# End of the second products: the folds of the row sums behind the last chunk's first four column blocks

## The chip, the cores and the metric

The kernel runs on one core of a Trainium2 chip. The metric is the device time of one execution in microseconds (us); where several runs are given, their median. A profile is one execution recorded by the hardware profiler. Engines: TensorE (PE; its weight loads are shown apart as PEld), VectorE (DVE), ScalarE (ACT), GpSimd (POOL), SyncE (SP). SP, ACT and POOL also issue DMA transfers, each into queues of its own.

## The reference

Two layers run over 256 tokens of 1024 channels. The change lies in the second half of a layer, a lookup of 16,384 small experts. Each of 8 heads chooses 16 experts for a token and gives each a gate; an expert is one row of `expert_down` (dot product with the token, then GELU) and one row of `expert_up` (scaled by the result and summed):

```python
        u = expert_down[experts]
        act = jax.nn.gelu(jnp.einsum('td,thkd->thk', t, u, preferred_element_type=jnp.float32),
                          approximate=False)
        wgt = (gate * act).astype(t.dtype)
        vv = expert_up[experts]
        return jnp.einsum('thk,thkd->td', wgt, vv)
```

The result times a modulation vector is added to the residual stream: `x = x + g2 * peer_ffn(...)`. Then the next layer starts with a norm and the product with `w_in`; behind layer 1, x is the output.

## The kernel before

**Dense and row tokens.** The first T tokens (`DENSE`: 168 in layer 0, 160 in layer 1) are computed densely, as if every expert were used, with zero gates for those not chosen. For the other TS = 88 or 96 tokens the chosen rows are fetched from memory by indirect DMA. `SETS` splits these tokens into sets of 64, 16 and 8 (layer 0) or 64 and 32 (layer 1).

**Second products.** `combine` (line 1165) makes the weighted sum of `expert_up`. `up` stands in 128 chunks of 128 experts by 1024 channels, 512 KB each, loaded in turn into a ring of 7 buffers (`raw`), odd chunks by SP's queue and even ones by ACT's. A chunk's product is eight matmuls in f32, one for each column block d of 128 channels: `add(i, d, u)` (line 1172) adds chunk i's block d for T tokens. The accumulators `acc` are four PSUM tiles; each holds two column blocks side by side, d and d + 1, of 256 columns each: T for the dense tokens, the rest for the row tokens. The profile shows two records for each f32 matmul on TensorE, and two weight loads.

**Row sums.** Meanwhile POOL fetches rows of `up` (line 1074), and DVE adds each, times its weight, to `R_SUM[s]` of its set (`add_row`, lines 1097 and 1099). A partition of `R_SUM[s]` holds a part of one token's rows. `folds(d)` (line 1176) sums these parts: for each set a matmul with block d of `R_SUM[s]` as weights and a constant 0/1 matrix `fold` of as many columns as the set has tokens (line 1179). It writes beside the dense tokens' columns in the same accumulator. The work is given out so that the last row is added, in program order, ahead of chunk 123.

**Order at the end.** The part is issued in the order in which it is written (`manual_schedule`), and every engine takes its instructions in that order. Chunks 0 to 125 run whole, chunk by chunk. Behind chunk 125 stand all eight `folds(d)` (lines 1212 to 1214): 24 matmuls in layer 0, 16 in layer 1. The last two chunks (`HELD` = 2) are loaded and kept in `last`; then, for each column block d, chunk 126's and chunk 127's matmuls follow one another (lines 1215 to 1217). At i = 127 of layer 0 two steps of the next layer's weights are taken (`cast_step`, a cast on ACT and, in one of them, a subtraction on DVE).

**Behind it.** `updates` (line 390) gives eight DVE operations, one for each d, which read acc and add the product with the gate to x (line 392). In layer 0 they are run at the start of the next layer's `bridge` (line 424): DVE updates x, ACT makes `R_U` and squares from it, and TensorE starts the next layer's products (`multiply`, line 446) with `R_U`. In layer 1 they are run at the very end (lines 1353 to 1357), with output DMAs from SP behind d = 3, 5, 6 and 7.

Of the kernel before, what the change touches and what calls it, by code (L numbers as in the profile page):

```python
# [20 lines left out]
DC = 8  # L21
# [39 lines left out]
ASIDES_UP = (4, 100)  # L61
F_FIRST = 4
F_LAST = 124
HELD = 2
FILL = 1.5
FILL_DOWN = (2.2, 2.1)
EARLY = (112, 116, 96, 100, 64, 68)
# [15 lines left out]
def hybrid_trunk(ctx: ExitStack, tc: tile.TileContext, x_in, c_in, vec_in, w_ada, w_in, w_out, w_pq,  # L83
# [164 lines left out]
    def cast_step(late=None):  # L248
        k = Src.cast
        if k >= len(Src.seq):  # L250
            return False
        dma_ahead(k + 1)
        while Src.later and Src.ring[Src.later[0][0]] <= Src.ring[k + 1] - 1 + RAW - QUEUE_LAG:
            nc.scalar.dma_start(*Src.later.pop(0)[1:])
        kind, _, arg = Src.seq[k]
        raw = raws.pop(k)
        Src.cast += 1
        if kind == "aside":
            Src.asides.append((k, lambda: ada_chunk(arg[0], arg[1], raw)))
        elif kind == "ada":  # L260
            ada_chunk(arg[0], arg[1], raw)
        elif kind in ("whole", "early", "second"):
            ready.append((raw, None))
        else:
            hi = stream.tile([P, D], F32R, name="hi", tag="hi", bufs=3)
            lo = stream.tile([P, D], F32R, name="lo", tag="lo", bufs=3)

            def low():
                if arg is None:
                    nc.vector.tensor_sub(lo, raw, hi.bitcast(F32))  # L270
                else:
                    nc.vector.scalar_tensor_tensor(lo, raw, arg, hi.bitcast(F32), op0=OP.mult,
                                                   op1=OP.subtract)

            with tc.high_priority(offset=AHEAD):
                if arg is None:
                    nc.scalar.copy(hi, raw)  # L277
                else:
                    nc.scalar.activation(hi, raw, AF.Copy, scale=arg)
                if late is None:  # L280
                    low()
                else:
                    late.append(low)
            ready.append((hi, lo))
        load_more(k)
        return True

    def run_aside(least=4):
        if Src.asides and Src.asides[0][0] <= Src.cast - least:
            Src.asides.popleft()[1]()  # L290
# [5 lines left out]
    def next_chunk(ahead=2, late=None):  # L296
        while len(ready) < 1 + ahead and cast_step(late):
            pass
        return ready.popleft()
# [71 lines left out]
    def bank(tag, bufs):  # L371
        return psum.tile([P, 512], F32, name=tag, tag=tag, bufs=bufs)
# [13 lines left out]
    def preload(func, after):  # L386

        nc.scalar.activation(spare, after, func, scale=0.0, bias=eps)  # L388

    def updates(acc, mod, g):  # L390

        return [lambda d=d: nc.vector.scalar_tensor_tensor(
            X[:, d, :], acc[d // 2][:, (d % 2) * S:(d % 2 + 1) * S], mod[:, g + d:g + d + 1], X[:, d, :],
            op0=OP.mult, op1=OP.add) for d in range(DC)]
# [125 lines left out]
    def tables(layer, after=None):  # L520
        if after is not None:
            for r in (R_BIAS, R_SW, R_SB):
                nc.scalar.copy(r[:, 0, 0:1], after)
        q = nc.gpsimd if layer == 0 else nc.sync
        q.dma_start(R_BIAS, rel_bias)
        q.dma_start(R_SW, sgu_w[layer])
        q.dma_start(R_SB, sgu_b[layer])
        return lambda: tables_rest(layer)
# [479 lines left out]
    def experts(layer, rest):  # L1008
# [59 lines left out]
        def fetch():  # L1068
            while free and len(held) < min(2 * TS, known_to[0]) and quota[0] > 0:
                quota[0] -= 1  # L1070
                n = len(held)
                k = n % TS
                held[n] = free.popleft()
                nc.gpsimd.indirect_dma_start(  # L1074
                    out=held[n], out_offset=None, in_=rows if n >= TS else down_rows[:, :],
                    in_offset=bass.IndirectOffsetOnAxis(ap=R_WHERE[:, k:k + 1].bitcast(U32), axis=0))
# [12 lines left out]
        def dot_acts(lo, hi):  # L1089
            nc.scalar.activation(R_DOTS[:, lo:hi], R_DOTS[:, lo:hi], AF.Gelu)  # L1090
            nc.vector.tensor_mul(R_DOTS[:, lo:hi], R_DOTS[:, lo:hi], pairs[:, 1, lo:hi])
# [73 lines left out]
        def combine(layer, late, dotted):  # L1165
            qg = None
            jobs = [(0, k) for k in range(dotted, TS)] + [(1, k) for k in range(TS)]
            acc = [bank("acc", 4) for _ in range(DC // 2)]
            added = 0
            last = []  # L1170

            def add(i, d, u):
                nc.tensor.matmul(acc[d // 2][:, (d % 2) * S:(d % 2) * S + T], u[:, d * P:(d + 1) * P], acts[:, i, :],  # L1173
                                 start=i == 0 and d % 2 == 0, stop=i == 127, skip_group_check=True)

            def folds(d):
                for s, (off, n) in enumerate(SETS):
                    at = (d % 2) * S + T + off
                    nc.tensor.matmul(acc[d // 2][:, at:at + n], R_SUM[s][:, d * P:(d + 1) * P], fold[layer][:, off:off + n],
                                     start=False, stop=True, skip_group_check=True)  # L1180

            free.extend(SLOTS_UP)
            fetch()
            for i in range(128):
                u = next_chunk()[0]
                while added < min(len(jobs), -(-len(jobs) * (i - F_FIRST + 1) // (F_LAST - F_FIRST))):
                    kind, k = jobs[added]
                    (add_row if kind else dot)(k)
                    added += 1
                    if not kind and k == TS - 1:  # L1190
                        dot_acts(dotted, TS)
                run_aside()
                if i == 126:
                    while Src.asides:
                        run_aside(1)
                if i == 127 and layer + 1 < DEPTH:
                    cast_step()
                    cast_step(late)
                if i >= 128 - HELD:
                    last.append((i, u))  # L1200
                else:
                    for d in range(DC):
                        add(i, d, u)
                if i == 120 and layer + 1 < DEPTH:
                    preload(AF.Sqrt, acts[:, i, 0:1])
                if i == 64 * S // T + 5:
                    nc.sync.dma_start(X.rearrange("p a b -> p (a b)"), x_dram)
                if i == 56 * S // T + 4 and layer + 1 < DEPTH:
                    others = tables(layer + 1)
                if i == 124 and layer + 1 < DEPTH:  # L1210
                    qg = others()
                if i == 125:
                    for d in range(DC):
                        folds(d)
            for d in range(DC):
                for i, u in last:
                    add(i, d, u)
            return updates(acc, mods[layer], G2), qg

        manual.enter_context(tc.manual_schedule())  # L1220
# [12 lines left out]
        start = None  # L1233
        for i in range(128):
# [46 lines left out]
            if start is None and shown == 2 and not lower:  # L1281
                start = i + 1
# [54 lines left out]
        if dotted < TS:  # L1337
            dot_acts(0, dotted)
        late = []
        update, qg = combine(layer, late, dotted)  # L1340
        return update, late, qg

# [95 lines left out]
```

## Time and profile before

| | |
|---|---|
| median of 3 runs | 1583.32 us (1582.72 to 1584.77) |
| the profiled execution, time | 1584.51 us |
| its span, first to last instruction | 1582.6 us |
| TensorE matmul / weight load busy | 1542.3 us (97%) / 1505.1 us (95%) |
| VectorE / ScalarE / GpSimd busy | 1000.0 / 472.5 / 496.8 us |
| memory read | 564.02 MB, 359 GB/s with what is written over the span |
| granted TensorE clock, mean | 0.991 of full |
| second products (L1173) | 4096 records, 580.5 us busy |
| folds (L1179) | 80 records, 48 in layer 0 and 32 in layer 1 |

How to read the views that follow. Times in a view count from the start of the span. The *chain of work that ended last* is followed back from the last instruction, at each step to what released it; a line is start, length, engine, tile, source line and how many instructions. The *timeline* lists instructions in order of time, like ones merged, with the idle time in front of them and what ended it in brackets. *Stretches* give, for a window, its length, then busy time and number of instructions of TensorE, its weight load, VectorE, ScalarE and, where it has any, GpSimd, then the granted TensorE clock (1.00 is full speed), the DMA engines' busy share and GB/s. *Groups* give engine, operation, output <- inputs, shape, count, then busy us and mean ns, then idle us before them. A *line's* view gives the shortest, median and longest duration in ns, then the first and the last start. In the *DMA queues*, q0 is the one of the row fetches, q1 is SP's and q10 is ACT's: packets, MB, share of the 16 engines' time. Matmuls overlap in TensorE's pipeline, so the pitch from one to the next is shorter than one's duration.

### The profile page before, as it was taken

To read this page: it belongs to the slowest core of one execution; us is meant where nothing else is said; L and a number is where in the kernel's file an instruction comes from. 1 tells how busy PE (TensorE), PEld (TensorE's weight loads), DVE (VectorE), ACT (ScalarE), POOL (GpSimd) and SP (SyncE) were. 2 spreads that over 40 slices of the span, in tenths; PEclk is the share of its full clock that TensorE was granted. 3 is DMA by queue.
4 is the path that set the end of the run, shared out by engine and by line. 5 is a ranking of instruction groups with operands and counts; after the bars stand their busy time and mean duration, and the time that the engine had idled before them with its cause. 6 is when DMAs were issued, how large, how long until landed. Compare 5 with 4: busy or idle time off the path is not lost.

```text
span 1582.6 us, 28957 instructions
## 1 busy us (share of the span) xinstructions
PE 1542.3 (97%) x11240; PEld 1505.1 (95%) x11240; DVE 1000.0 (63%) x2255; ACT 472.5 (30%) x1356; POOL 496.8 (31%) x424
## 2 busy tenths in 40 slices
PE   6999999999999999998999999999999999999997
PEld 5879999999999999998999899999999999999997
DVE  6778898677787444444337578877667754444434
ACT  2346313465553000000026663134656610000000
POOL 1000124334344434444200001245443334444441
PEclk9999999999999999999999999999999999999998
DMA  9998489999999999999955574899999999999995
GB/s 385 339 375 319 138 289 348 418 418 419 417 418 416 415 419 419 418 419 419 412 189 171 186 258 139 292 351 419 417 418 419 418 419 419 418 419 419 419 418 211
DMA packets 156681, 571.21 MB, mean 361 GB/s; under 512 B 18131, under 2 KB 18659, under 8 KB 155392
## 3 DMA queue, kind: packets, MB, share of 16 engines
q1 hardware_dynamic: 66096, 241.07, 39.7%
q0 software_dynamic: 55744, 202.36, 32.0%
q10 hardware_dynamic: 34704, 125.93, 19.9%
q8 instruction: 88, 1.44, 0.3%
q14 instruction: 49, 0.40, 0.1%
HBM read 564.02 MB, written 4.09 MB: 359 GB/s over the span
## 4 chain that ended last, share of the span: by engine, by line
PE 40%; DMA 38%; issue 8%; DVE 7%; POOL 4%; ACT 2%; ACTq 0%; POOLq 0%; SPq 0%; DVEq 0%
DMA arena<-in_up,arena 17%; PE acc L1173 17%; DMA arena<-in_down_rows,arena 12%; PE ch L357 9%; DMA spots<-in_down_rows,arena 3%; DMA raw<-in_up 3%; POOL arena L1074 3%; PE ch L359 2%; PE ch L360 2%; PE ch L361 2%; DVE raw L227 1%; DMA raw<-in_w_ada 1%; PE ch L446 1%; DVE arena L1084 1%; PE g L952 1%
## 5 line engine op out<-in xcount | busy, mean ns | idle before, releaser
L1173 PE MATMUL acc<-arena,raw 128*128 128x168 f32 (+1 forms) x4096 | 580.5, 305 | 9.0 <-DMA raw<-in_up 9.0
L1173 PEld LDWEIGHTS acc<-arena,raw 128*128 128x128 f32 x4096 | 577.6, 192 | 11.3 <-DMA raw<-in_up 11.2
L357 PE MATMUL ch<-arena,raw 128*128 128x168 f32 (+2 forms) x3776 | 560.7, 307 | 0.1
L357 PEld LDWEIGHTS ch<-arena,raw 128*128 128x128 f32 x3776 | 536.2, 190 | 5.6 <-issue 1.8
L1099 DVE SCALAR_TENSOR_TENSOR spots<-arena,spots 128x1024 f32<-128x1024 f32 x156 | 200.4, 1284 | 222.1 <-DMA arena<-in_up,arena 220.8
L1074 POOL DMA_INDIRECT arena<-in_up,arena x159 | 215.1, 1353 | 280.5 <-DMA arena<-in_up,arena 203.9
L1074 POOL DMA_INDIRECT arena<-in_down_rows,arena x151 | 178.3, 1181 | 242.9 <-DVE arena L1084 180.7
L1084 DVE SCALAR_TENSOR_TENSOR arena<-arena,spots 128x1024 f32<-128x1024 f32 x151 | 183.1, 1222 | 86.1 <-DMA arena<-in_down_rows,arena 79.6
L1117 ACT ACTIVATE arena<-arena,parts 128x128 f16<-128x128 f16 x164 | 64.6, 394 | 142.1 <-DVE arena L1107 102.5
L388 ACT ACT_TABLE_LOAD x6 | 7.7, 1283 | 284.9 <-PE acc L1173 284.8
L357 PE MATMUL ch<-arena 128*128 128x160 f32 (+2 forms) x544 | 86.0, 317 | 6.1 <-issue 3.6
L357 PEld LDWEIGHTS ch<-arena 128*128 128x128 f32 x544 | 79.8, 192 | 11.2 <-ACT arena L410 5.2
L1150 ACT ACTIVATE arena<-ch 128x336 f32<-128x336 f32 (+32 forms) x122 | 41.9, 343 | 149.4 <-PE ch L357 128.9
L227 DVE SCALAR_TENSOR_TENSOR aside<-aside,arena 128x1024 f32<-128x1024 f32 x48 | 58.6, 1220 | 43.9 <-DMA aside<-in_w_ada 43.8
L359 PE MATMUL ch<-hh,hi 128*128 128x256 f32 x288 | 82.6, 289 | 2.0 <-DVE arena L477 1.9
L360 PE MATMUL ch<-hh,lo 128*128 128x256 f32 x288 | 81.8, 284 | 0.0
L361 PE MATMUL ch<-hh,hi 128*128 128x256 f32 x288 | 81.7, 284 | 0.0
L270 DVE TENSOR_TENSOR lo<-raw,hi 128x1024 fp32r<-128x1024 f32 x42 | 51.2, 1225 | 37.3 <-ACT hi L277 36.3
L227 DVE SCALAR_TENSOR_TENSOR raw<-raw,arena 128x1024 f32<-128x1024 f32 x48 | 57.9, 1217 | 8.9 <-DMA raw<-in_w_ada 5.4
L1119 ACT ACTIVATE arena<-arena,parts 128x128 f16<-128x128 f16 x164 | 63.4, 387 | 0.0
L1123 ACT ACTIVATE arena<-arena,parts 128x128 f16<-128x128 f16 x164 | 63.4, 386 | 0.0
L1121 ACT ACTIVATE arena<-arena,parts 128x128 f16<-128x128 f16 x164 | 63.4, 386 | 0.0
(231 smaller groups left out, 1661.9 us busy)
## 6 DMA issues: line engine op xcount, KB each, us to landing
raw<-in_up SPq DMA_DIRECT2D x128, 512.0 KB
raw<-in_up ACTq DMA_DIRECT2D x128, 512.0 KB
raw<-in_down SPq DMA_DIRECT2D x114, 512.0 KB
raw<-in_down ACTq DMA_DIRECT2D x112, 512.0 KB
raw<-in_w_ada SPq DMA_DIRECT2D x48, 512.0 KB
aside<-in_w_ada SPq DMA_DIRECT2D x48, 512.0 KB
raw<-in_w_pq SPq DMA_DIRECT2D x32, 512.0 KB
arena<-in_down SPq DMA_DIRECT2D x30, 512.0 KB
```

Of the source, the lines that this page charges most:

```text
L227: nc.vector.scalar_tensor_tensor(raw, raw, 1.0, cact, op0=OP.mult, op1=OP.mult, accum_out=mods[layer][:, col:col + 1])
L357: nc.tensor.matmul(dst, hi[:, cols], k[0], start=start, stop=stop, **kw)
L359: nc.tensor.matmul(dst, hi[:, cols], k[0], start=start, stop=False, **kw)
L360: nc.tensor.matmul(dst, lo[:, cols], k[0], start=False, stop=False, **kw)
L361: nc.tensor.matmul(dst, hi[:, cols], k[1], start=False, stop=stop, **kw)
L1074: nc.gpsimd.indirect_dma_start(out=held[n], out_offset=None, in_=rows if n >= TS else down_rows[:, :], in_offset=bass.IndirectOffsetOnAxis ...
L1084: nc.vector.scalar_tensor_tensor(row, row, 1.0, R_DX[which(k)[0]], op0=OP.mult, op1=OP.mult, accum_out=R_DOTS[:, k:k + 1])
L1099: nc.vector.scalar_tensor_tensor(R_SUM[s], row, w, R_SUM[s], op0=OP.mult, op1=OP.add)
L1117: nc.scalar.activation(og[0][:, 0, i, :], oh[:, 0, i, :], AF.Copy, scale=parts[:, 0, t + i:t + i + 1])
L1119: nc.scalar.activation(og[1][:, 0, i, :], oh[:, 0, i, :], AF.Copy, scale=parts[:, 1, t + i:t + i + 1])
L1121: nc.scalar.activation(og[0][:, 1, i, :], oh[:, 1, i, :], AF.Copy, scale=parts[:, 0, t + 2 + i:t + 3 + i])
L1173: nc.tensor.matmul(acc[d // 2][:, (d % 2) * S:(d % 2) * S + T], u[:, d * P:(d + 1) * P], acts[:, i, :], start=i == 0 and d % 2 == 0, stop= ...
```

## The change

Chunks 126 and 127 are no longer held. Chunk 126 runs whole like those before it. Chunk 127 runs block by block; behind its blocks d = 4 to 7 stands `folds(d - 4)`, so behind block 4 the fold of block 0, and so on (`FOLD_LAG` = 4). Behind the last block stand `folds(4)` to `folds(7)`. The number of matmuls, their operands and shapes, the DMAs and the order of the other engines' instructions stay; the closing flag of an accumulation (`stop`) moves from the last chunk's matmuls to the folds alone, which now are the last to write each accumulator.

```diff
-HELD = 2
+FOLD_LAG = 4
...
-            last = []
-
             def add(i, d, u):
                 nc.tensor.matmul(acc[d // 2][:, (d % 2) * S:(d % 2) * S + T], u[:, d * P:(d + 1) * P], acts[:, i, :],
-                                 start=i == 0 and d % 2 == 0, stop=i == 127, skip_group_check=True)
+                                 start=i == 0 and d % 2 == 0, stop=False, skip_group_check=True)
...
-                if i >= 128 - HELD:
-                    last.append((i, u))
-                else:
-                    for d in range(DC):
-                        add(i, d, u)
+                for d in range(DC):
+                    add(i, d, u)
+                    if i == 127 and d >= FOLD_LAG:
+                        folds(d - FOLD_LAG)
...
-                if i == 125:
-                    for d in range(DC):
-                        folds(d)
-            for d in range(DC):
-                for i, u in last:
-                    add(i, d, u)
+            for d in range(DC - FOLD_LAG, DC):
+                folds(d)
```

## The prediction, made before the changed kernel was run

> **What bounds the kernel now.** I read the chain of work that ended last first, cut to the end of each layer's second products, then the timeline there, then the clock by stretches. Layer 0 of the two layers, chain (start us, us, what):
>
> ```profile
> 810.49 6.41 PE acc L1179 x48
> 816.90 6.82 PE acc L1173 x32
> 823.72 4.34 PE ch L446 x20
> ```
>
> Layer 1, the same view:
>
> ```profile
> 1564.33 1.30 DVE spots L1099
> ...
> 1565.67 6.61 PE acc L1179 x30
> 1572.28 6.09 PE acc L1173 x32
> ...
> 1578.40 0.48 DVE arena L392
> ```
>
> Both ends are a run of folds (L1179), then the 16 matmuls of the two held chunks (32 records: each f32 matmul leaves two), then the updates (L392). In layer 0, TensorE has no gap: it is the bound. In layer 1 the folds wait for DVE's last row sum. Timeline of layer 1:
>
> ```profile
> 1557.73 7.89 DVE L1099 SCALAR_TENSOR_TENSOR spots<-arena,spots 128x1024 f32<-128x1024 f32 x6 [0.30 <-DMA arena<-in_up,arena]
> ...
> 1560.83 0.33 PE L1179 MATMUL acc<-fold,spots 128*128 128x64 f32 x2
> ...
> 1565.67 6.61 PE L1179 MATMUL acc<-fold,spots 128*128 128x32 f32 x30 [4.51 <-DVE spots L1099]
> ```
>
> The first fold of the 64-token set goes at 1560.83, the first of the 32-token set stands 4.51 us, and both held chunks stand behind it. Last, busy time by stretch; after the POOL column comes the granted clock, then DMA share and GB/s:
>
> ```profile
> 810.33:814.35 4.02, 4.02 (x39) 4.02 (x38) 1.22 (x1) 2.19 (x3) 0.00 (x0) 1.00 0.66 217
> 814.35:821.17 6.82, 6.82 (x29) 6.82 (x29) 0.88 (x2) 1.26 (x3) 0.00 (x0) 0.50 0.19 68
> ...
> 1561.86:1565.27 3.41, 0.00 (x0) 0.00 (x0) 3.34 (x3) 0.00 (x0) 0.00 (x0) 1.00 0.07 29
> ...
> 1565.67:1572.00 6.33, 6.33 (x30) 6.33 (x30) 0.00 (x0) 0.00 (x0) 0.00 (x0) 0.50 0.00 0
> 1572.28:1578.37 6.09, 6.08 (x32) 5.84 (x32) 2.63 (x6) 0.00 (x0) 0.00 (x0) 0.73 0.07 29
> ```
>
> This is the second half of the price: the clock is at half through most of both ends. In layer 1 it falls behind an empty stretch of 3.41 us. In layer 0 it falls with TensorE busy, behind a stretch of folds alone. By shape, first the stretch before that fall (810.94 to 814.35), then one before another fall (749.50 to 752.91), then one after which the clock stayed (230.67 to 234.09); behind them, as before, two stretches with their clock:
>
> ```profile
> L1179 PE MATMUL acc<-fold,spots 128*128 128x64 f32 x11 | 2.4, 297 | 0.0
> L1179 PE MATMUL acc<-fold,spots 128*128 128x8 f32 x12 | 2.2, 256 | 0.0
> L1179 PE MATMUL acc<-fold,spots 128*128 128x16 f32 x10 | 1.7, 248 | 0.0
> ...
> L1173 PE MATMUL acc<-arena,raw 128*128 128x168 f32 x9 | 1.6, 323 | 2.5 <-DMA raw<-in_up 2.5
> ...
> L357 PE MATMUL ch<-arena 128*128 128x168 f32 x13 | 2.4, 312 | 1.6 <-issue 1.6
> ```
>
> ```profile
> 752.91:756.32 3.41, 3.41 (x15) 3.41 (x14) 1.28 (x1) 0.00 (x0) 1.43 (x1) 0.50 1.02 419
> 810.94:814.35 3.41, 3.41 (x33) 3.41 (x33) 1.22 (x1) 1.71 (x3) 0.00 (x0) 1.00 0.65 205
> ```
>
> A wide record costs 0.1427 us for 168 columns at full clock (1104 records below), 0.85 ns a column. So the folds' stretch streamed 11 x 64 + 12 x 8 + 10 x 16 = 960 columns, 0.82 of 3.41 us, a share of 0.24; the second 9 x 168 = 1512, 0.38; the third 2184, 0.54. My reading: the clock goes by streamed columns, and falls below a share somewhere between 0.38 and 0.54. This is an inference from few stretches.
>
> [...]
>
> **Costs.** Nothing is computed more or less: 80 fold records and 64 late records of chunks are moved. The speeds:
>
> ```profile
> 509.63 157.55 PE acc L1173 x1104
> ...
> 1524.83 36.16 PE L1173 MATMUL acc<-arena,raw 128*128 128x160 f32 x265
> ```
>
> At full clock an add record costs 157.55 / 1104 = 0.1427 us in layer 0 and 36.16 / 265 = 0.1365 in layer 1; a fold record 4.02 / 39 = 0.103 in layer 0. At half clock layer 1's folds cost 6.42 / 30 = 0.214 (1565.67 to the 1572.09 of the next group), so 0.107 at full. I take 0.105: the cost hardly follows the columns.
>
> *Layer 0.* Are the operands there? The row sums: the last add ends at 796.99. The chunks, by the last loads' issue, by the first weight cast of the next layer, which comes behind chunk 127 in the same queue, and by the DMA queues from 806 on:
>
> ```profile
> 795.71 1.28 DVE L1099 SCALAR_TENSOR_TENSOR spots<-arena,spots 128x1024 f32<-128x1024 f32 x1 [1.53 <-DMA arena<-in_up,arena]
> ...
> 810.45 1.04 ACT L277 CAST hi<-raw 128x1024 fp32r<-128x1024 f32 x1 [13.93 <-DMA raw<-in_w_in]
> ...
> L213 SPq DMA_DIRECT2D raw<-in_up x1: 328/328/328, 796.8 to 796.8; - x1
> L254 ACTq DMA_DIRECT2D raw<-in_up x1: 334/334/334, 801.4 to 801.4; - x1
> ...
> q1 hardware_dynamic: 652, 2.34, 40.2%
> ```
>
> From 806 to 824 the only traffic to speak of is SP's queue (q1), so ACT's (q10, chunk 126) had nothing left; in SP's queue, that of chunk 127, a later load had landed at 810.45. New order from 810.33: 32 add records x 0.1427 = 4.57, 48 fold records x 0.105 = 5.04, in all 9.6 us, to 819.9, if the clock stays. Now it is 13.39 us, to 823.72: gain 3.8. The 6.82 us at half clock are worth 3.41 by themselves; I take 3.6. What follows: the updates.
>
> ```profile
> 819.38 0.88 DVE L392 SCALAR_TENSOR_TENSOR arena<-acc,mod,arena 128x256 f32<-128x256 f32 x2 [6.63 <-PE acc L1173]
> ...
> 823.76 0.88 DVE L392 SCALAR_TENSOR_TENSOR arena<-acc,mod,arena 128x256 f32<-128x256 f32 x2 [0.26 <-PE acc L1173]
> ```
>
> They run in pairs, one pair to an accumulator, the last pair right behind TensorE's end. In the new order pair (0,1) is free after fold 1, four blocks early as now, and pair (6,7) after the last fold: the same shape, 3.6 us earlier, so the next layer's first products (L446) move with it. Released buffers: chunk 126's comes free at about 812.6 and not past 816, so SP issues further loads of the next layer earlier; DMA then stands still, as the row shows, so nothing collides and I count no gain.
>
> ```profile
> 816.90:823.72 6.82, 6.82 (x33) 6.82 (x34) 2.63 (x6) 2.98 (x8) 0.00 (x0) 0.69 0.00 0
> ```
>
> *Layer 1.* The row sum is done at 1565.63 as before (DVE and row fetches are untouched). Chunks landed? DMA queues from 1557 to 1566:
>
> ```profile
> q0 software_dynamic: 422, 1.51, 41.2%
> q10 hardware_dynamic: 4, 0.01, 0.2%
> ```
>
> Only row fetches (q0) move after 1557; ACT's queue has 4 packets left, SP's none: both chunks are there. From 1560.83: chunk 126 takes 16 records x 0.1365 = 2.18, chunk 127's blocks 0 to 4 take 10 x 0.1365 = 1.37, the first fold's 64-token part 0.21, to 1564.6; then TensorE waits about 1.0 us for the row sum. This is the wait that the change moves: queued behind it on TensorE are three blocks and the folds, and only the updates wait for these. From 1565.67: 30 fold records x 0.105 = 3.15 and 6 add records = 0.82, to 1569.6. Now it is 1578.37: gain 8.8 on TensorE. The stretch 1561.86 to 1565.27 is then mostly wide matmuls, so the fall at 1565.27 goes with its cause.
>
> ```profile
> 1576.22 0.88 DVE L392 SCALAR_TENSOR_TENSOR arena<-acc,mod,arena 128x256 f32<-128x256 f32 x2 [0.74 <-PE acc L1173]
> 1577.13 2.60 SPq L1357 DMA_DIRECT2D out_t<-arena  x4
> 1577.31 0.88 DVE L392 SCALAR_TENSOR_TENSOR arena<-acc,mod,arena 128x256 f32<-128x256 f32 x2 [0.21 <-PE acc L1173]
> ```
>
> The output starts behind update 3 (pair (2,3) ends at 1577.10). New: fold 3 ends at 1565.67 + 0.21 + 3 x (0.27 + 0.42) = 1567.95, its pair at about 1568.85: 8.25 earlier. Three pairs of 0.88 then stand back to back on DVE, the last ending at 1570.65, where now it ends at 1578.40 + 0.88 = 1579.28: 8.6. I take 8.3, the output's own length unchanged.
>
> **Sum:** 3.6 + 8.3 = 11.9 us. Off the profiled execution's own 1584.51 (its span is 1582.6) that is 1572.6; it lies 1.2 over the median of the runs, 1583.32, off which it is 1571.4. I take **1572.0**, between the two. Bounds of the unknown: the gain is 11.65 to 12.4 by the ends above, before the clock.
>
> **Rivals.**
>
> *One fall of the clock is left in layer 0.* The tail is 24 fold records alone, 2.5 us, before L446. A stretch of 3.41 us ending at the last fold has the tail (0.24) and one block with its fold (0.285 of adds, 0.63 of folds: 0.47), in all 0.30: a fall, if a window ends there. One ending a microsecond before or after is over 0.35, and where the windows lie is not set by the kernel as far as I can see. Price 3.41 / 2 = 1.7: 1573.7. [...]
>
> *Layer 0's part is lost*: the fold tail and the mixed blocks (share 0.47, inside my uncertain band) together hold the clock at half for two windows as now (3.41 lost), or the 3.6 us are waited for again in layer 1's DMA-bound stage. For: the band; against: that stage's loads start when layer 1's products release buffers, so they should move along. 11.9 - 3.6 = 8.3 left: 1575.6.
>
> *The last chunks are not there in layer 1* and TensorE waits for them instead. The latest that they can have landed is the end of all traffic:
>
> ```profile
> 1564.00:1565.00 1.00, 0.00 (x0) 0.00 (x0) 0.00 (x0) 0.00 (x0) 1.00 0.00 0
> ```
>
> From 1564.0, 32 add records (4.37) and 32 folds (3.36) end at 1571.7, not 1569.6: 1574.1. Against: the queue rows above.
>
> *Slower:* a fold between adds of the same accumulator does not overlap its neighbours.
>
> ```profile
> L1179 PEld LDWEIGHTS acc<-fold,spots x80: 190/306/338, 810.2 to 1571.8; 128*128 128x128 f32 x80
> L1179 PE MATMUL acc<-fold,spots x80: 219/352/454, 810.3 to 1571.9; 128*128 128x64 f32 x32, 128*128 128x16 f32 x16, 128*128 128x8 f32 x16, 128*128 128x32 f32 x16
> ```
>
> The ends for a fold record in the new place: 0.105, its pitch now, and 0.352, its whole median length. A weight load hidden under the add before it could also bring it below 0.105; the nearest such row, a wide record of 0.1427, has its own load hidden, and the folds' matmuls are too short to hide one, so I exclude a large gain. At 0.352, 48 + 30 records x 0.247 = 19.3 us: 1591.3. It decides from 0.105 + 11.9 / 78 = 0.26 us a record. Against: now adds of two chunks to the same columns follow each other without a gap, and so do three folds. I take 0.105, the pitch of the same instruction.
>
> **How the numbers follow.** Forecast 0.52, one fall 0.23, layer 0 lost 0.14, chunks late 0.04, slower 0.03, and 0.04 for what I have not seen, near no change. The range 1569.9 to 1575.8 reaches from the largest gain off the median, 1583.32 - 12.4 = 1570.9, less half the spread of the runs (1582.72 to 1584.77), to the loss of layer 0's part. About 0.2%, 3.2 us, can be told from no change: faster 0.94, within 0.03, slower 0.03.
>
> **What would show it.** In the chain, L1179 and L1173 mixed at both ends; granted clock 1.00 from 810 to the updates and from 1560 to the end of TensorE's work; about 1 us of wait for DVE L1099 in layer 1, not 4.5; from 810.33 (or its like) 9.6 us to L446; span near 1570.7. Clock at 0.50 in layer 0's tail shows the first or second rival; a wait for raw<-in_up the third; fold records further apart than 0.105 the last. The forecast is wrong if layer 1's start of the output moves by less than 8 us, or if layer 0's gain is not found again at the start of layer 1's second products.

## The result, and the profile after

The changed kernel takes 1573.74 us (median of 4 runs, 1573.04 to 1575.54); the kernel before, run beside it, 1584.05 us (4 runs, 1582.72 to 1585.47). The ratio is 0.9939 with a 95% interval of 0.9924 to 0.9954: 10.3 us less. Two later comparisons gave 0.9964 (0.9952 to 0.9977) and 0.9936 (0.9918 to 0.9953), so 5.6 and 9.5 us by their medians.

The profiled execution of the changed kernel spans 1571.1 us, before 1582.6. In its listing the adds stand on line 1171 and the folds on line 1177. The chain of work that ended last, layer 0:

```profile
769.96 41.33 PE acc L1171 x290
811.28 0.57 PE acc L1177 x6
811.85 0.39 PE acc L1171 x2
...
814.15 3.25 PE acc L1177 x30
817.40 6.13 PE ch L446 x20
...
```

Adds and folds alternate as the change says, and TensorE has no gap. But the 20 records of L446 now take 6.13 us, where they took 4.34 before. The clock by stretch shows why (windows of 3.41 us around the end of the folds; the granted clock is the third number from the end):

```profile
814.62:818.03 3.41, 3.41 (x29) 3.33 (x30) 2.35 (x6) 2.77 (x9) 0.00 (x0) 1.00 0.53 161
818.03:821.44 3.41, 3.41 (x10) 2.67 (x9) 3.41 (x10) 1.28 (x4) 0.00 (x0) 0.50 0.00 0
```

Of the 6.82 us at half clock before, 3.41 are left, moved from the folds to the next layer's first products. That is the first rival of the prediction, not its forecast. The forecast's sign, a granted clock of 1.00 from 810 to the updates, is not met.

In layer 1, from the timeline:

```profile
1554.24 6.67 DVE L1099 SCALAR_TENSOR_TENSOR spots<-arena,spots 128x1024 f32<-128x1024 f32 x5 [1.67 <-DMA arena<-in_up,arena]
...
1562.07 0.53 PE L1177 MATMUL acc<-fold,spots 128*128 128x64 f32 x4
...
1564.22 2.31 PE L1177 MATMUL acc<-fold,spots 128*128 128x64 f32 x20
1564.79 2.66 DVE L392 SCALAR_TENSOR_TENSOR arena<-acc,mod,arena 128x256 f32<-128x256 f32 x6 [0.56 <-PE acc L1177]
1565.69 2.32 SPq L1350 DMA_DIRECT2D out_t<-arena  x4
```

The last row sum is done at 1554.24 + 6.67 = 1560.91 and the first fold comes at 1562.07: in this execution TensorE does not wait at all. It came late, because it had waited for a chunk at the start of layer 1's second products, with a half-clock window behind it (timeline, then stretches):

```profile
1280.50 8.86 PE L1171 MATMUL acc<-arena,raw 128*128 128x160 f32 x64
1291.61 270.62 PE L1171 MATMUL acc<-arena,raw 128*128 128x160 f32 x1978 [2.26 <-DMA raw<-in_up]
```

```profile
1285.00:1295.00 10.00, 7.74 (x49) 7.50 (x48) 4.72 (x5) 0.00 (x0) 4.53 (x4) 0.87 1.03 417
1295.00:1305.00 10.00, 10.00 (x72) 10.00 (x72) 5.88 (x5) 0.00 (x0) 6.37 (x6) 0.96 1.03 415
```

Was that wait a price of the change? Did layer 0's gain reach the end? Is it the narrow folds that make the clock fall? The experiments ask these. Two measures serve throughout:

- **Layer 0's end:** from the end of chunk 125 to the end of L446's 20 records; it holds the folds, chunks 126 and 127 and these records, and nothing else. Before: 810.49 to 828.06, 17.57 us. Changed: 811.28 to 823.53, plus the 26 add records of chunks 126 and 127 ahead of the first fold, 26 x 0.1427 = 3.71: 15.96.
- **Layer 1's end:** from the last row sum to the end of the span. Before: 1565.63 to 1582.6, 17.0 us. Changed: 1560.91 to 1571.1, 10.2 us.

### The profile page after: what moved, and what is told of

Its sections match the earlier page's. It is cut to its first block, busy times and chain, and to the rows that moved or that the text cites. A ratio compares the mean times of both kernels' runs of the same rounds, so it can differ in the third digit from the quotient of the medians.

```text
span 1571.1 us, 28958 instructions
## 1 busy us (share of the span) xinstructions
PE 1535.6 (98%) x11240; PEld 1499.7 (95%) x11240; DVE 999.2 (64%) x2255; ACT 472.0 (30%) x1356; POOL 496.4 (32%) x424
## 4 chain that ended last, share of the span: by engine, by line
PE 72%; DMA 13%; issue 6%; DVE 4%; POOL 3%; ACT 2%; ACTq 0%; SPq 0%; POOLq 0%; DVEq 0%; another core or an unknown queue 0%
PE acc L1171 33%; PE ch L357 22%; DMA arena<-in_down_rows,arena 6%; DMA raw<-in_up 4%; POOL arena L1074 3%; PE ch L359 2%; PE ch L360 2%; PE ch L361 2%; PE g L1133 1%; DMA spots<-in_down_rows,arena 1%; DMA raw<-in_w_ada 1%; PE ch L446 1%; DVE raw L227 1%; PE g L952 1%; PE acc L360 1%
```

## The experiments

### The changed kernel again, and each layer alone

> The changed kernel once more. Theory A (the ends of the two layers carry the gain, and the wait of 2.3 us for chunk 4 at the start of layer 1's second products is a variation from run to run): again 10 to 11 us below the kernel before, with that wait sometimes there and sometimes not; one half-clock window of 3.4 us at the end of layer 0 in most executions. Theory B (the earlier start of layer 1 brings that wait with it): the wait of about 2.3 us at chunk 4 is there again, with a fall of the clock behind it.

Measured: 1576.64 us against 1582.22, ratio 0.9964 (0.9952 to 0.9977), 5.6 us, not the 10 to 11 that theory A expected. The wait at chunk 4 was not there, nor in the second repeat below; theory B falls for it. In its place stands the wait for the row sum, from the timeline of this run:

```profile
1562.92 0.33 PE L1177 MATMUL acc<-fold,spots 128*128 128x64 f32 x2
1565.13 0.41 PE L1177 MATMUL acc<-fold,spots 128*128 128x32 f32 x2 [1.88 <-DVE spots L1099]
```

The last row sum ends at 1565.09, the span at 1574.1: 9.0 us for layer 1's end. So the row sum is the bound in this execution. In the first profile TensorE came 1.2 us late for it (layer 1's end 10.2 us instead of 9.0): the early wait there took the place of this late one, and cost little beyond it.

> The new order in layer 0 alone; layer 1 keeps the folds behind chunk 125 and the held pair. Theory A: only layer 0's end is gained, 1.6 us with one fall of the clock on the next layer's first products, 3.4 us without, so 1.5 to 3.5 us below the kernel before; layer 1's end shows the wait for the last row sum and a half clock as before. Theory B: layer 0's gain is given back at layer 1's chunk 4 (2 to 3 us), so no difference within 1 us.

What differs from the changed kernel in this run and the next (here `NEW` = 0, there 1), cut to the order of the work:

```diff
-                for d in range(DC):
-                    add(i, d, u)
-                    if i == 127 and d >= FOLD_LAG:
-                        folds(d - FOLD_LAG)
+                if layer != NEW and i >= 128 - HELD:
+                    last.append((i, u))
+                else:
+                    for d in range(DC):
+                        add(i, d, u)
+                        if layer == NEW and i == 127 and d >= FOLD_LAG:
+                            folds(d - FOLD_LAG)
...
-            for d in range(DC - FOLD_LAG, DC):
+                if layer != NEW and i == 125:
+                    for d in range(DC):
+                        folds(d)
+            for d in range(DC - FOLD_LAG if layer == NEW else DC, DC):
                 folds(d)
+            for d in range(DC):
+                for i, u in last:
+                    add(i, d, u)
```

Measured: 1583.04 us against 1582.22, ratio 1.0 (0.9991 to 1.001, 11 runs). The time says B; the profiled execution (1580.18 us, one of the faster ones) does not. Its chain at layer 0's end:

```profile
810.81 0.57 PE acc L1181 x6
...
813.67 3.25 PE acc L1181 x30
816.92 6.13 PE ch L448 x20
```

With 3.71 us of adds ahead of 810.81 that is 15.95 us, 1.6 less than before. From there, 823.05, to the last row sum (1561.05) it is 738.0 us; before it was 737.6 and in a second profile of the kernel before (below) 738.0. So in this execution the layers' middle is not longer, and layer 0's gain is still there at the last row sum.

> The new order in layer 1 alone; layer 0 as before. Theory A: from the start of chunk 125 to the end of the span about 14.7 us instead of 23.9, so 8 to 9.5 us below the kernel before. Theory B: the same, and no wait at chunk 4 of layer 1, since layer 0 is as before; with B the gains of this run and of the run with layer 0 alone add up to the whole, with layer 0's part near zero.

Measured: 1577.73 us against 1582.22, ratio 0.9961 (0.9946 to 0.9976), with single runs from 1571.22 to 1581.66: 4.5 us by the medians, where A had 8 to 9.5. The profiled one is the slowest of them, and shows the layer 1 end that A left out, with a 2.33 us wait for the row sum inside one clock window:

```profile
1564.64:1568.05 3.41, 1.08 (x10) 0.94 (x8) 2.97 (x3) 0.00 (x0) 0.00 (x0) 1.00 0.03 12
1568.05:1571.46 3.41, 3.41 (x17) 3.41 (x16) 0.87 (x2) 0.00 (x0) 0.00 (x0) 0.51 0.00 0
```

TensorE was busy for 1.08 of 3.41 us, and everything behind ran at half clock: 12.0 us from the row sum (1567.69) to the end (1579.7), not 9.0. The change shortens the wait, but a rest of 2.33 us still cost 3 us of clock here; the 1.88 us of the first repeat did not.

### What makes the clock fall in layer 0

> The kernel before, with one matmul of 168 columns added behind each of layer 0's 24 folds (same weights, result unused). At full clock that is 48 more records of 0.1427 us, 6.85 us; the stretch from the first fold to the next layer's first product becomes 48 x 0.105 + 80 x 0.1427 = 16.5 us instead of 13.4. Theory A (the clock falls because the folds stream few columns; with the wide ones the share is about 0.67): the clock stays at 1.00 there, about 3 us slower than the kernel before. Rival (the fall belongs to the end of the part, whatever TensorE streams): the fall is there, 3.4 us more, about 6.5 us slower.

```diff
+            wide = bank("g", 2) if layer == 0 else None
...
+                    if layer == 0:
+                        nc.tensor.matmul(wide[:, :T], R_SUM[s][:, d * P:(d + 1) * P], acts[:, 125, :], start=True,
+                                         stop=True, skip_group_check=True)
```

Measured: one run of 1584.49 us; the kernel before beside it 1581.7, so 2.8 us slower. Stretches from the first fold to L446:

```profile
807.87:811.28 3.41, 3.41 (x29) 3.41 (x28) 1.23 (x1) 2.18 (x3) 0.00 (x0) 1.00 0.72 235
...
814.70:818.11 3.41, 3.41 (x29) 3.41 (x28) 0.00 (x0) 0.00 (x0) 0.00 (x0) 1.00 0.01 2
818.11:821.52 3.41, 3.41 (x28) 3.41 (x27) 0.11 (x1) 0.00 (x0) 0.00 (x0) 1.00 0.00 0
821.52:824.63 3.11, 3.11 (x24) 3.11 (x24) 2.51 (x6) 2.70 (x8) 0.00 (x0) 1.00 0.00 0
```

The clock is full throughout, with the DMA engines standing still as before. The stretch from 807.87 to 824.63 is 16.8 us where A had 16.5 and the rival 19.9. TensorE is 100% busy in both kernels; what differs is the columns that it streams. So in these runs the fall (granted clock 0.50 before, 1.00 with the wide matmuls) went with a run of narrow folds alone, not with the end of the part, with standing DMA engines or with TensorE's busy time.

> The changed kernel with every fold of layer 0 right behind its own block (lag 0); layer 1 keeps lag 4. The tail of 24 folds alone is gone; the stretch of chunk 127 with its folds has a share of streamed columns of 0.47 for 7 us. If the clock falls only below a share of about 0.4: no fall in layer 0, 1.7 us below the changed kernel. If it falls above 0.47: a fall inside the stretch, one or two windows, equal to the changed kernel or up to 1.7 us slower.

```diff
-FOLD_LAG = 4
+FOLD_LAG = (0, 4)
...
-                    if i == 127 and d >= FOLD_LAG:
-                        folds(d - FOLD_LAG)
+                    if i == 127 and d >= FOLD_LAG[layer]:
+                        folds(d - FOLD_LAG[layer])
...
-            for d in range(DC - FOLD_LAG, DC):
+            for d in range(DC - FOLD_LAG[layer], DC):
                 folds(d)
```

Measured: 1574.63 us against 1584.52, ratio 0.9939 (0.9921 to 0.9957); the changed kernel in the same comparison 1575.03. By time nothing is told apart. The chain of its layer 0:

```profile
811.28 0.57 PE acc L1177 x6
811.85 0.39 PE acc L1171 x2
...
817.97 0.57 PE acc L1177 x6
818.54 4.44 PE ch L446 x20
```

With the 18 add records ahead of the first fold (2.57 us) that is 822.98 - 811.28 + 2.57 = 14.27 us, 1.7 less than changed, and L446 is back at 4.44 us: no fall (granted clock 1.00 from 811.10 to 821.30). By shapes, one window of 3.41 us inside this stretch (814.51 to 817.92), and, from the second repeat of the changed kernel below, the window of its tail (815.50 to 818.91), behind which the clock fell (0.51 from 818.91 to 822.33):

```profile
L1171 PE MATMUL acc<-arena,raw 128*128 128x168 f32 x8 | 2.1, 348 | 0.0
L1177 PE MATMUL acc<-fold,spots 128*128 128x8 f32 x8 | 1.5, 256 | 0.0
L1177 PE MATMUL acc<-fold,spots 128*128 128x64 f32 x8 | 1.3, 247 | 0.0
L1177 PE MATMUL acc<-fold,spots 128*128 128x16 f32 x6 | 1.0, 249 | 0.0
```

```profile
L1177 PE MATMUL acc<-fold,spots 128*128 128x64 f32 x10 | 2.0, 281 | 0.0
L1177 PE MATMUL acc<-fold,spots 128*128 128x8 f32 x10 | 1.9, 265 | 0.0
L1177 PE MATMUL acc<-fold,spots 128*128 128x16 f32 x10 | 1.7, 249 | 0.0
L1171 PE MATMUL acc<-arena,raw 128*128 128x168 f32 x2 | 0.5, 348 | 0.0
```

At 0.85 ns a column (the prediction's 0.1427 us for 168) these are 2016 columns, a share of 0.50, and 1216, a share of 0.30. TensorE is busy without a gap in both (3.41 of 3.41 us). The closest case is the first profile of the changed kernel, with the window shown above (814.62 to 818.03), behind which the clock fell too:

```profile
L1177 PE MATMUL acc<-fold,spots 128*128 128x8 f32 x9 | 1.7, 256 | 0.0
L1177 PE MATMUL acc<-fold,spots 128*128 128x64 f32 x8 | 1.7, 288 | 0.0
L1177 PE MATMUL acc<-fold,spots 128*128 128x16 f32 x8 | 1.4, 249 | 0.0
L446 PE MATMUL ch<-arena,raw 128*128 128x257 f32 x4 | 1.3, 453 | 0.0
```

These are 1740 columns, a share of 0.43. The count takes every record whole that reaches into the window, so it is good to a few hundredths only.

### A layer 0 without a narrow tail

> Layer 1 as in the changed kernel. In layer 0 the folds stand behind chunks 123 to 125, three, three and two, and the last two chunks are held and run block by block, so that no stretch of folds alone and no narrow tail is left. If the clock goes by streamed columns (share 0.65 in the mixed chunks), it stays at full speed to the end of the next layer's first products: 1.7 us below the changed kernel. If the fall at the end of layer 0 has another cause (the end of the part, DMA standing still), it is there again and the time is that of the changed kernel.

```diff
-                if layer != NEW and i == 125:
-                    for d in range(DC):
+                if layer != NEW and 123 <= i <= 125:
+                    for d in range(DC)[3 * (i - 123):3 * (i - 122)]:
                         folds(d)
```

(Against the kernel with the new order in layer 1 alone: `NEW` = 1, and for layer 0 the held pair as in the kernel before.) Measured: 1572.5 us against 1582.22, ratio 0.9931 (0.9919 to 0.9944); the changed kernel beside it had 0.9964 (0.9952 to 0.9977). Its chain:

```profile
805.16 1.91 PE acc L1181 x18
...
814.98 4.66 PE acc L1175 x32
819.64 4.34 PE ch L448 x20
```

805.16 to 823.98 less the 32 records of chunks 124 and 125 (4.57) is 14.25 us: the full clock (1.00 in every stretch from 804.98 to 823.80), 1.7 us below the changed kernel, as A said. The medians differ by 4.1 us, more than that, so it was run again beside the changed kernel.

> The changed kernel once more, to be compared with the next three on one chip. Theory A (one fall of 3.4 us on the next layer's first products in layer 0; a wait of 0 to 2.5 us for the last row sum in layer 1, with or without a fall behind it; 0 to 4 us lost near 1085 us in every kernel): 6 to 10 us below the kernel before.

> Layer 0's folds spread over chunks 123 to 125, layer 1 as changed, once more. Theory A: layer 0 keeps its full clock, so 1.7 us below the changed kernel in the mean; the 4 to 5 us of the first comparison were mostly the varying spot near 1085 us. Rival (the spread does more than save one window, since it makes layer 1 start at another place): again 4 to 5 us below.

Measured: changed 1575.03 us, spread 1573.8, against 1584.52; ratios 0.9936 (0.9918 to 0.9953) and 0.9937 (0.9919 to 0.9955). In the profiles the differences are again those of A: layer 0's end 15.94 (changed) and, from the same lines as above, 14.25 (spread), layer 1's end 9.0 in both. In the time of whole executions, which vary by 5 us and more, 1.7 us does not show in this comparison; the rival's 4 to 5 us are not there.

> The kernel before, but in layer 0 the folds behind chunks 123 to 125, three, three and two, with the last two chunks held as before; layer 1 as before. No fall of the clock at layer 0's end: 3.4 us gained there. Theory A: the gain reaches the end, about 3.4 us faster. Theory B (layer 0's gain is absorbed in layer 1, as the run with the new order in layer 0 alone suggests): no difference within 1 us.

Measured: 1580.09 us against 1581.7, ratio 0.9987 (0.9978 to 0.9996): 1.6 us gained by the medians; the interval reaches from 0.6 to 3.5, so it leaves out theory B's zero and does not leave out A's 3.4. The chain has 14.25 us for layer 0's end and 737.6 us from there to the last row sum, as before.

### Layer 1: the wait alone, and a longer lag

> The kernel before without the last six row sums of layer 1 (the outputs of the row tokens lack them), so that the folds there wait for nothing; order as before. Theory A (the wait costs its own 4.5 us and the half clock behind it): from 126 chunks on, 32 fold records of 0.105 and 32 add records of 0.1365, 7.7 us to the end of TensorE's work instead of 17.5, or up to 1.7 more if a window falls on the folds: 8 to 10 us faster. Rival (the wait costs only itself, and the order is what keeps the clock): 4.5 us faster, with the clock at half through folds and adds.

```diff
-                    (add_row if kind else dot)(k)
+                    if not (layer == 1 and kind and k >= TS - 6):
+                        (add_row if kind else dot)(k)
```

Measured: one run of 1576.9 us (the kernel before 1581.7). In this execution layer 0 had three windows of half clock instead of two, and its end took 19.2 us, so the whole run is 4.8 us faster and not 8 to 10, and the reading goes by layer 1. Chain:

```profile
1544.90 17.93 PE acc L1173 x132
1562.83 3.49 PE acc L1179 x32
1566.32 4.44 PE acc L1173 x32
...
```

From the first fold (1562.67 in the timeline) to the end of the span (1575.0) it is 12.3 us; in the kernel before, 1560.83 to 1582.6, 21.8. The wait was 4.5 us and its removal gains 9.4: the other half was the clock, as A said (1.00 here from 1562.67 to 1566.08 and from 1566.32 to 1570.45; before, 0.50 on the folds and 0.73 on the adds). In these two executions the old order with nothing to wait for is as fast as the new one: the changed kernel's profile, which had no wait either, has 12.6 us from the same point (1562.07 less 26 x 0.1365 to 1571.1).

> Layer 0 spread, and in layer 1 all folds behind chunk 127 (lag 8), so that three blocks more are done when TensorE comes to wait for the last row sum. Theory A: from the last row sum 30 fold records and no adds, 3.2 us instead of 4.0 to the end of TensorE's work where that sum is the bound: 0.8 us below the run with layer 0 spread alone, if no window of half clock falls on the folds; with one, up to 1.6 us more, so that it may be slower.

```diff
-FOLD_LAG = 4
+FOLD_LAG = 8
```

(Against the kernel with layer 0 spread.) Measured: 1573.77 us, ratio 0.9933 (0.9917 to 0.995), the same time as lag 4. The timeline of its layer 1 shows the wait down to 0.29 us, and the end follows 8.2 us behind the row sum (1561.21 to 1569.4), 0.8 less than lag 4:

```profile
1560.63 0.33 PE L1181 MATMUL acc<-fold,spots 128*128 128x64 f32 x2
1561.25 3.54 PE L1181 MATMUL acc<-fold,spots 128*128 128x32 f32 x30 [0.29 <-DVE spots L1101]
```

No half clock fell on its 30 folds in this execution: they took 3.54 us, where 30 took 6.61 in the kernel before.

### How much the kernel before varies

> The kernel before, for a second profile. Theory A (layer 1's first products give a varying length of half clock around 1085 us, 3.4 or 6.8 us, in every kernel): the ends of the layers as in the first profile, 13.4 us from first fold to the next layer and 23.9 us from chunk 125 to the end, give or take a window; the half clock near 1085 may be 6.8 instead of 3.4. Theory B (the earlier start of layer 1 makes it longer): 3.4 again.

Measured: one run of 1582.85 us. Layer 0's end 17.55 us (808.83 to 826.38), layer 1's 16.5 (1564.37 to 1580.9). One stretch, 1080 to 1100, in this profile, then in the first one of the kernel before:

```profile
1080.00:1100.00 20.00, 16.44 (x109) 15.38 (x109) 17.77 (x35) 12.16 (x42) 12.62 (x10) 0.83 1.02 413
```

```profile
1080.00:1100.00 20.00, 17.99 (x135) 16.98 (x133) 16.93 (x34) 10.84 (x38) 11.25 (x10) 0.91 1.03 419
```

The clock there is 0.83 and 0.91; it is 1.00 in the run with lag 8 in layer 1. The kernel before has both lower values; theory B falls here too. In the two profiles of the changed kernel that followed the first it was 0.83, in the first 0.91.

## Why the prediction was right, and where it was not

The measured 1573.74 us lies in the range (1569.9 to 1575.8) and is within 0.1 us of the first rival (1573.7); the forecast of 1572.0 was 1.7 us low. That it comes so close is luck in part: the two later comparisons put the changed kernel at 1576.64, outside the range, and at 1575.03 us, and 3 of the 11.5 us that the first profile is shorter are none of the change (see the sum, below).

**Layer 0: the term was mis-sized, by the step "if the clock stays".** 3.6 us were forecast; 1.6 came. The costs of the records were right: where the clock stays (lag 0, spread), the end takes 14.25 us and the gain is 3.3; the rest to 3.6 lies in the adds beside folds, which are a little dearer (a mixed block takes 0.96 us instead of 0.92). But one window of half clock is left, 1.7 us by the prediction's own price, on the first products behind the narrow tail. It was there in all four profiles with this order in layer 0 (changed three times, layer 0 alone once; the chains of three of them have 6.03 to 6.13 us for L446's 20 records, where the kernel before had 4.34), where the prediction gave it 0.23. The reading behind it, that the clock goes by streamed columns, held in the run made for it: with wide matmuls added to the folds the clock stayed at 1.00. By the same count of columns the band of 0.38 to 0.54 narrows from both sides in these runs: the changed kernel's tail fell at 0.43, and a window of 1984 columns (0.49) in the lag 8 run's tail stayed at full clock,

```profile
L1181 PE MATMUL acc<-fold,spots 128*128 128x64 f32 x11 | 2.3, 282 | 0.0
L1181 PE MATMUL acc<-fold,spots 128*128 128x32 f32 x10 | 1.9, 267 | 0.3 <-DVE spots L1101 0.3
L1175 PE MATMUL acc<-arena,raw 128*128 128x160 f32 x6 | 1.0, 299 | 0.0
```

so the mixed blocks (0.47 by the forecast, 0.50 counted) kept the clock and the tail did not.

The chance of 0.23 did not follow from that reading. The half clock began 0.6 us behind the end of the folds in the first profile (818.03 against 817.40) and 0.3 us ahead of it in the second repeat (818.91 against 819.19), and was there in both. Slide a window of 3.41 us over the changed kernel's own records, 0.85 ns a column, and at about three quarters of its places the share is under 0.38, at which the kernel before had fallen already (an estimate from the profile beside the result). So the fall was the likely case and should have been the forecast.

**Layer 1: right in mechanism and size where the row sum is the bound.** 8.3 us were forecast; from the row sum to the end it is 9.0 instead of 17.0, so 8.0, in two repeats, in both spread runs and in the lag 0 run (with the old order it is 16.5 to 17.9 in five profiles). The wait left was put at 1.0 us; it was 0.6 to 2.3 us in six profiles with this order, and 4.4 to 5.3 in the five with the old one. In the profile beside the result it was 0, since TensorE was late, and the gain there was 17.0 - 10.2 = 6.8. The prediction's own sign, that the output starts 8 us earlier, is met from the span's start (1577.13 to 1565.69); from the row sum on it is 6.7 us there and 7.95 in the first repeat (its output starts at 1568.64), so it is just missed. Its other sign, layer 0's gain found at the start of layer 1's second products, is met: from the end of L446's 20 records to there it is 457.0 us, before 457.7. That "the fall goes with its cause" was too much: with 2.33 us of wait left it came back once and cost 3 us. The run without the last row sums shows what the order does: it hides the wait behind the last chunks, and was worth nothing in the execution that had no wait.

**The rivals.** *Chunks late:* no execution waited for chunk 126 or 127. *Slower, by folds that do not overlap:* 0.57 us for six fold records, 0.095 each, below the 0.105 taken, with the adds beside them at 0.39 for two instead of 0.285. *Layer 0's part lost:* no profile shows it; from layer 0's end to the last row sum it is 735.9 to 740.1 us in the thirteen profiles that have this sum, and neither order stands apart. But the timed runs with layer 0 alone changed gained less than the profiles say: 0 (up to 1.4 us) instead of 1.6, and 1.6 instead of 3.3, which the interval (0.6 to 3.5) just holds. This is not settled; parts that vary in every kernel, such as the stretch near 1085 us, hide sizes like these.

**The sum.** 11.5 us less span in the profile beside the result is 1.6 in layer 0 and 6.8 in layer 1; the other 3 us are none of the change, since they lie ahead of it: its first add starts 1.1 us earlier (508.4 against 509.5, by the lines' views), and chunk 125 of layer 0 ends another 1.8 us earlier relative to that (811.28 - 3.71 - 508.4 = 299.2 against 810.49 - 509.5 = 301.0). A usual execution has 1.6 + 8.0 = 9.6 us, and the three comparisons gave 10.3, 5.6 and 9.5.

The version with layer 0's folds spread over chunks 123 to 125 was below the changed kernel in the first comparison (0.9931 against 0.9964, intervals apart) and equal in the second; its 1.7 us in layer 0 stand in every profile of it.

## What to carry to other kernels

A wait and a run of small matmuls at the end of a stage cost twice here: their own time, and the half clock behind them (4.5 us of wait cost 9.4; the tail of folds cost 1.7 us more on the next layer's products). So try small matmuls mixed among wide ones, which kept the clock here (14.25 us for layer 0's end, not 15.96), and no tail of them, also ahead of the next stage, which paid for it. And when a wait is moved, look for what ends last at the new place: here the row sums still did, so an earlier stall of TensorE (2.26 us, and a window at half clock) cost 1.2 us at the end.

## What the runs showed of the hardware

The windows here are 3.41 us long; the share is what their records stream of the columns that wide adds stream in that time (0.85 ns each). TensorE's clock fell to half with the engine busy for 3.41 of 3.41 us behind shares of 0.24 (the kernel before, 810.94 to 814.35), 0.30 (the second repeat, 815.50 to 818.91) and 0.43 (the changed kernel, 814.62 to 818.03). It stayed full at 0.50 (the lag 0 run, 814.51 to 817.92) and 0.49 (the lag 8 run, 1560.00 to 1563.41; all 30 folds in 3.54 us). TensorE's busy time does not sort these windows. In the lag 0 run it was busy for 1.55 us of one, waiting for a chunk, and the clock stayed full behind it; its 11 x 168 columns are a share of 0.46:

```profile
749.59:753.00 3.41, 1.55 (x11) 1.55 (x12) 3.34 (x3) 0.00 (x0) 1.02 (x2) 1.00 1.03 420
753.00:756.41 3.41, 3.41 (x27) 3.41 (x26) 1.47 (x2) 0.00 (x0) 2.13 (x2) 1.00 1.03 420
```

```profile
L1171 PE MATMUL acc<-arena,raw 128*128 128x168 f32 x11 | 1.8, 315 | 2.5 <-DMA raw<-in_up 2.5
```

The kernel before had nine such records in such a window (0.38; TensorE busy for 1.37 us, 749.50 to 752.91), and its clock was 0.50 behind it. Nor did weight loads keep the clock up: in the changed kernel's window of 0.43 they were busy for 3.33 of 3.41 us. In layer 1 of the kernel before the fall came behind a window with TensorE idle (0.00 of 3.41 us), in its layer 0 behind one without a gap, and with wide matmuls beside the same folds the clock was 1.00 from 807.87 to 824.63. That the clock goes by the columns is the author's reading of these windows; at which share it turns, and how other shapes and types count, was not shown.
